# The end of cross attention and the first SwiGLU products, taken in halves of the tokens

## The chip, the cores and the metric

The kernel runs on one core of a Trainium2 chip. The metric is the time of one execution in device microseconds (us). A core has five engines with queues of their own, each of which takes its instructions strictly in its own order: TensorE (PE; its weight loads are listed as PEld), VectorE (DVE), ScalarE (ACT), GpSimd (POOL) and SyncE (SP), which issues most transfers.

## The reference, cut to what matters

Two layers act on 1024 tokens of 1024 features. Each layer is a mixer, then cross attention into 256 memory tokens, then a SwiGLU network of width 2816, each with a root-mean-square norm ahead and a residual add behind. The change is at the seam between the last two.

```python
def rms_norm(x, g):
    y = xf * lax.rsqrt(jnp.mean(xf * xf, axis=-1, keepdims=True) + EPS)
    return (y * g.astype(jnp.float32)).astype(x.dtype)
...
    x = x + memory_cross_attention(rms_norm(x, g_xa[layer]), m, ...)     # ends in  o @ w_o
    x = x + swiglu(rms_norm(x, g_ffn[layer]), w_gate[layer], w_up[layer], w_down[layer])
...
def swiglu(h, w_gate, w_up, w_down):
    return (jax.nn.silu(h @ w_gate) * (h @ w_up)) @ w_down
```

## The kernel before, in words

**Layout.** The residual stream is kept transposed: eight chunks `x[m]` of 128 features (partitions) by 1024 tokens. A fp32 matrix is split in a rounded high part and a low part (`h` and `l`), and a product is three matmuls: high by high, high by low, low by high. The high part is a ScalarE cast (L306 for the activations, L242 for weights), the low part a VectorE subtraction (`low`, L433). "Matmul" below means one such instruction on 128x128 weights and 512 columns.

**SwiGLU in seven products.** Gate and up are done by a seven-product scheme on 2x2 blocks (`seven`, L1749). A `Pair` (L278) holds two neighbouring chunks; its blocks are b11 and b12 (first and second 512 tokens of the even chunk) and b21 and b22 (of the odd one). It yields seven operands: 0 is b11, 1 is b21, 6 is b22, and 2 to 5 are differences of blocks, made by four GpSimd subtractions (L296). A `Unit` is the like for a 1024x256 piece of weights. One product is 12 matmuls: four pairs by three. A gate unit and an up unit are 14 products, and 11 such couples follow each other in a layer.

**The seam.** Cross attention ends in `project(1, m)` (L1660), for chunk after chunk: 12 matmuls for both halves of the tokens, and two VectorE adds onto `x[m]` (L1666). `x_part` (L1722) then makes, for each half, a scaled copy g*x on ScalarE (L1730), which the pair's blocks are taken from, a square on ScalarE (L1734, L1737), and on GpSimd the sum of squares over the chunks (L1738). When a chunk has both halves it is stored to DRAM (L1742) and its buffer is freed. A pair is ready when both of its chunks are through. After product 0 of the first gate unit, `stats` turns the sum of squares into 1/rms with 8 one-column products on TensorE, and `spread` broadcasts it over the partitions. It is needed only where a product's output is gated.

**What sets the order.** A planner (`run`, L447) walks a list of tasks. It makes operands ahead of their task, in the order of first use, as far as a look-ahead in columns (`la`) and room in two SBUF arenas allow; `lead` puts the operands of three pairs ahead of the first product. A scheduler below it then sets each engine's own order. Transfers are issued by SyncE in order.

## Time and profile before

| | before |
|---|---|
| median of 3 runs | 2464.09 us (2460.8 to 2465.05) |
| profiled execution: time, span | 2464.76 us, 2463.0 us |
| TensorE busy | 2355.2 us (96%) |
| VectorE, ScalarE, GpSimd busy | 1729.0 (70%), 1023.0 (42%), 747.0 us (30%) |
| mean granted TensorE clock | 0.977 |

The profiled execution is within 0.7 us of the median, so sums made on its span carry over. A share is a mean over the run: stages differ, and a stage is read from its own stretch. A granted clock of 1.00 is TensorE's upper level of 2.4 GHz, 0.50 the lower of 1.2 GHz; a value between is a mean over the stretch.

### The profile page before, as it was taken

Reading aid. Unit: us, or ns where it says so; the run is one execution under the profiler, and the core shown is the slowest. Engines: PE = TensorE matmul, PEld = TensorE weight load, DVE = VectorE, ACT = ScalarE, POOL = GpSimd, SP = SyncE. Lnnn points to the kernel's source line nnn. Section 1 sums busy time; section 2 is a strip of 40 time slices with the busy share of each in tenths; the row PEclk is TensorE's granted clock in tenths of the full one; section 3 lists DMA queues with packets and bytes.
Section 4 is the critical chain, followed back from the end, with each engine's and each line's share of the span. In section 5 each row is a group of like instructions: output and inputs, shape, how many; then the busy total and the mean of one; then the engine's idle time right before and its main releaser. Section 6 shows DMA issues by size and latency. Waiting matters only on the chain. (4 is left out here: it accounts for less than half of the span.)

```text
span 2463.0 us, 30890 instructions
## 1 busy us (share of the span) xinstructions
PE 2355.2 (96%) x11246; PEld 1973.7 (80%) x11246; DVE 1729.0 (70%) x2501; ACT 1023.0 (42%) x1858; POOL 747.0 (30%) x721
## 2 busy tenths in 40 slices
PE   7999999999899999998999999999799999998999
PEld 7998889888668888776887888888577887876887
DVE  5456467855789988877668653455888889877765
ACT  5355356745544444442224221244544444442221
POOL 6541233343454334241001310142642334331000
PEclk9999999999989999999999999999799999999999
DMA  7345344421214434459762121120314434359773
GB/s 231 125 134 190 95 120 129 129 95 35 103 52 171 154 137 143 165 177 361 261 228 92 57 77 35 35 69 18 120 52 163 149 137 159 133 198 380 235 245 99
DMA packets 249345, 350.24 MB, mean 142 GB/s; under 512 B 13120, under 2 KB 151448, under 8 KB 249192
## 3 DMA queue, kind: packets, MB, share of 16 engines
q1 hardware_dynamic: 245360, 335.46, 41.5%
q0 software_dynamic: 3648, 12.75, 1.4%
q8 instruction: 88, 1.44, 0.2%
q14 instruction: 65, 0.53, 0.1%
q10 hardware_dynamic: 184, 0.05, 0.0%
HBM read 233.78 MB, written 114.43 MB: 141 GB/s over the span
## 5 line engine op out<-in xcount | busy, mean ns | idle before, releaser
L421 PE MATMUL psum_t<-arena_r 128*128 128x512 f32 (+4 forms) x10304 | 2278.4, 380 | 86.3 <-DVE arena_r L433 34.3
L421 PEld LDWEIGHTS psum_t<-arena_r 128*128 128x128 f32 (+1 forms) x10304 | 1863.5, 190 | 451.1 <-DVE arena_r L433 54.2
L433 DVE TENSOR_TENSOR arena_r<-arena_f,arena_r 128x512 fp32r<-128x512 f32 (+4 forms) x811 | 702.8, 886 | 183.1 <-ACT arena_r L242 49.5
L242 ACT CAST arena_r<-arena_f 128x512 fp32r<-128x512 f32 (+2 forms) x504 | 284.0, 584 | 464.1 <-PE psum_t L421 259.0
L1839 POOL TENSOR_TENSOR arena_f<-arena_f 128x512 f32<-128x512 f32 x88 | 164.4, 1875 | 497.5 <-ACT arena_f L1838 497.5
L233 DVE TENSOR_TENSOR arena_f<-arena_f 128x512 f32<-128x512 f32 (+2 forms) x288 | 211.0, 736 | 85.5 <-DMA arena_f<-w_down 52.6
L1818 DVE TENSOR_TENSOR arena_f<-psum_t,arena_f 128x512 f32<-128x512 f32 x224 | 148.1, 684 | 59.3 <-PE psum_t L421 58.6
L1864 ACT CAST arena_r<-arena_f 128x512 fp32r<-128x512 f32 x154 | 95.5, 621 | 197.6 <-DVE arena_f L1846 70.4
L1860 POOL TENSOR_TENSOR arena_f<-arena_f 128x512 f32<-128x512 f32 x88 | 144.0, 1657 | 73.8 <-DVE arena_f L1846 72.1
L1787 DVE TENSOR_TENSOR arena_f<-psum_t,arena_f 128x512 f32<-128x512 f32 x176 | 119.7, 683 | 36.8 <-PE psum_t L421 23.7
L665 POOL TENSOR_TENSOR arena_f<-arena_f 128x1024 f32<-128x1024 f32 x21 | 60.9, 2898 | 273.9 <-ACT arena_f L661 176.0
L551 ACT CAST arena_r<-arena_f 128x1024 fp32r<-128x1024 f32 (+1 forms) x57 | 59.0, 1042 | 114.4 <-PE psum_t L421 97.7
L433 DVE TENSOR_TENSOR arena_r<-psum_t,arena_r 128x512 fp32r<-128x512 f32 (+3 forms) x124 | 84.6, 703 | 23.3 <-ACT arena_r L1653 7.3
L1838 ACT ACTIVATE arena_f<-arena_f 128x512 f32<-128x512 f32 x88 | 55.6, 632 | 83.6 <-DVE arena_f L1837 83.5
L1292 POOL TENSOR_SCALAR arena_f<-arena_f,small 128x640 f32<-128x640 f32 (+6 forms) x64 | 49.5, 782 | 108.7 <-DVE small L1291 104.7
L1846 DVE TENSOR_TENSOR arena_f<-arena_f 128x512 f32<-128x512 f32 x88 | 77.1, 876 | 4.9 <-POOL arena_f L1839 1.2
L444 POOL TENSOR_TENSOR small<-small,mhalf 128x4 f32<-128x4 f32 (+1 forms) x64 | 63.2, 987 | 5.2
L1837 DVE TENSOR_TENSOR arena_f<-arena_f 128x512 f32<-128x512 f32 x88 | 63.3, 720 | 0.1
L1738 POOL TENSOR_TENSOR arena_f<-arena_f 128x512 f32<-128x512 f32 x28 | 43.0, 1551 | 50.6 <-ACT arena_f L1737 50.2
L1287 ACT ACTIVATE arena_f<-psum_t,small 128x640 f32<-128x640 f32 (+6 forms) x64 | 47.5, 744 | 23.2 <-DVE small L1285 20.2
L296 POOL TENSOR_TENSOR arena_f<-arena_f 128x512 f32<-128x512 f32 x32 | 50.8, 1605 | 11.5 <-PE psum_t L421 7.4
L2031 POOL TENSOR_TENSOR arena_f<-arena_f 128x1024 f32<-128x1024 f32 x4 | 10.4, 2601 | 139.6 <-DVE arena_f L1983 134.7
(178 smaller groups left out, 1426.7 us busy)
## 6 DMA issues: line engine op xcount, KB each, us to landing
pq<-arena_r SPq DMA_DIRECT2D x154, 512.0 KB
arena_r<-pq SPq DMA_DIRECT2D x308, 256.0 KB
arena_f<-w_gate SPq DMA_DIRECT2D x22, 1024.0 KB
arena_f<-w_up SPq DMA_DIRECT2D x22, 1024.0 KB
arena_f<-xs SPq DMA_DIRECT2D x32, 512.0 KB
arena_r<-qk SPq DMA_DIRECT2D x48, 256.0 KB
xs<-arena_f SPq DMA_DIRECT2D x24, 512.0 KB
arena_f<-w_down SPq DMA_DIRECT2D x12, 1024.0 KB
```

What stands on the lines that cost most here:

```text
L233: getattr(T.nc, self.adds).tensor_tensor(out=out, in0=a, in1=b, op=what)
L242: T.nc.scalar.copy(out=hv, in_=src)
L421: self.nc.tensor.matmul(out=out, lhsT=lhsT, rhs=rhs, start=start, stop=stop, skip_group_check=again)
L433: getattr(self.nc, eng).tensor_tensor(out=out, in0=src, in1=high, op=ALU.subtract)
L444: self.nc.gpsimd.tensor_tensor(out=out, in0=in_, in1=self.mhalf[:, 0:in_.shape[-1]], op=ALU.pow)
L1787: nc.vector.tensor_tensor(out=o, in0=bank[q].ap, in1=o if other is None else other, op=ALU.add)
L1818: nc.vector.tensor_tensor(out=o, in0=bank[q].ap, in1=o, op=ALU.add)
L1837: nc.vector.tensor_tensor(out=q, in0=q, in1=r, op=ALU.mult)
L1839: nc.gpsimd.tensor_tensor(out=q, in0=q, in1=r, op=ALU.mult)
L1846: nc.vector.tensor_tensor(out=c[j].ap[:, o], in0=c[j].ap[:, o], in1=s.ap[:, o], op=ALU.mult)
L1860: nc.gpsimd.tensor_tensor(out=out, in0=a, in1=b, op=ALU.subtract)
L1864: nc.scalar.copy(out=t.ap[:, 0:512], in_=src)
```

## The change

**Cross attention.** The eight `project(1, m)` are done for the first 512 tokens of all chunks, then for the second 512 (6 matmuls each). `x_final` takes the place of `x_part`. Each half of a chunk is stored by its own transfer, 16 a layer instead of 8, of half the bytes. There is no scaled copy. For a first half, x is scaled in place on GpSimd (after its store has read it), and the sum of squares still runs on GpSimd. For a second half, x stays unscaled, its square goes into four one-column products on TensorE, which write to a PSUM bank of their own.

**Operands.** Operands 0 and 1 of a pair need only the two first halves, the other five need the second halves too. The two first differences are made on VectorE, in an instruction that multiplies by g and subtracts, two others stay on GpSimd; operand 6 is scaled in its cast (ScalarE) and its low part (VectorE).

**Order of the first couple.** Products 0 and 1 of gate and up come first (48 matmuls), then the statistics, then the other ten. The look-ahead is 16384 columns over the seam instead of 3072 and then 2048.

```diff
 class Pair:
+    def ready(self, i):
+        return self.lo[i] if i < 2 else all(self.hi)
...
     def make(self, T, i, h, l):
...
         if i == 2:
-            self.t1, self.t2 = T.F.get(512, "ba"), T.F.get(512, "ba")
-            op(self.t1.ap, b12, b11)
-            op(self.t2.ap, b22, self.t1.ap)
+            nc.vector.scalar_tensor_tensor(out=t1, in0=x12, scalar=self.g[0], in1=b11,
+                                           op0=ALU.mult, op1=ALU.subtract)
+            nc.vector.scalar_tensor_tensor(out=t2, in0=x22, scalar=self.g[1], in1=t1,
+                                           op0=ALU.mult, op1=ALU.subtract)
         if i == 4:
-            op(b12, b22, b12)
+            nc.gpsimd.tensor_tensor(out=t1, in0=t2, in1=b11, op=ALU.subtract)
         if i == 5:
-            op(b21, b21, self.t2.ap)
+            nc.gpsimd.tensor_tensor(out=t2, in0=b21, in1=t2, op=ALU.subtract)
+        if i == 6:
+            nc.scalar.activation(out=h.ap, in_=x22, func=AF.Copy, scale=self.g[1])
+            nc.vector.scalar_tensor_tensor(out=l.ap, in0=x22, scalar=self.g[1], in1=h.f,
+                                           op0=ALU.mult, op1=ALU.subtract)
...
-        for m in range(8):
-            self.add(lambda m=m: project(1, m, wo[1][m // 4]), [wo[1][m // 4]])
+        def tail():
+            self.la, self.f_reserve = 16384, 1024
+        self.add(tail)
+        for half in range(2):
+            if half:
+                self.add(lambda: setattr(self, "f_reserve", 4096))
+            for m in range(8):
+                self.add(lambda m=m, half=half: project(1, m, wo[1][m // 4], (half,)), [wo[1][m // 4]])
...
-    def x_part(self, pairs, gname, layer, m, half):
+    def x_final(self, pairs, layer, m, half):
...
+        nc.sync.dma_start(out=self.xs[m * P:(m + 1) * P, c], in_=x)
+        if half:
+            pr.hi[e] = True
...
+            def sums():
+                for b in range(4):
+                    self.mm(self.sums.ap[:, m * 4 + b:m * 4 + b + 1], sq.ap[:, b * P:(b + 1) * P],
+                            self.ones[:, 0:1], True, True)
...
+        def scale():
+            nc.gpsimd.tensor_scalar(out=x, in0=x, scalar1=pr.g[e], scalar2=1.0, op0=ALU.mult, op1=ALU.mult)
+            pr.lo[e] = True
+        self.defer(scale, 2)
...
+                lead = [p.ops[i] for p in pairs[:2] for i in (2, 3, 6, 4, 5)]
+                gt = self.seven(g, pairs, self.collected(later(gated)), lead)
+                ut = self.seven(u, pairs, self.collected(later(upped(0))))
+                self.tasks += gt[:2] + ut[:2]
+                self.add(lambda: (self.half_stats(), self.spread()))
+                self.tasks += gt[2:]
+                self.add(steady)
+                self.tasks += ut[2:]
```

**TensorE, layer 0, from the last transposes of cross attention on.** Before (`128x1` are the one-column products of the statistics, `arena_f,ones` the broadcast):

```order
L421 MATMUL psum_t<-arena_r 128x512 x159
L421 MATMUL psum_t<-ones,arena_f 128x1 x4
L421 MATMUL psum_t<-arena_r 128x512 x4
L421 MATMUL psum_t<-ones,arena_f 128x1 x4
L421 MATMUL psum_t<-arena_r 128x512 x11
L421 MATMUL psum_t<-arena_f,ones 128x512 x2
L421 MATMUL psum_t<-arena_r 128x512 x2813
```

And now:

```order
L442 MATMUL psum_t<-arena_r 128x512 x122
L442 MATMUL psum_t<-ones,arena_f 128x1 x4
L442 MATMUL psum_t<-arena_r 128x512 x5
L442 MATMUL psum_t<-ones,arena_f 128x1 x4
L442 MATMUL psum_t<-arena_r 128x512 x20
L442 MATMUL psum_t<-ones,arena_f 128x1 x8
L442 MATMUL psum_t<-arena_r 128x512 x38
L442 MATMUL psum_t<-ones,arena_f 128x1 x8
L442 MATMUL psum_t<-arena_r 128x512 x13
L442 MATMUL psum_t<-ones,arena_f 128x1 x12
L442 MATMUL psum_t<-arena_r 128x512 x42
L442 MATMUL psum_t<-arena_f,ones 128x512 x2
```

Four batches of 12 more matmuls stand ahead of the statistics, and 32 one-column products are spread among them where there were none.

**VectorE, layer 0, from the first adds of `project(1, m)` on.** L1666 is now L1696 (add onto x), L433 is now L454 (low part), L313 and L323 are the new scaled subtractions. Before:

```order
L1666 TENSOR_TENSOR arena_f<-psum_t,arena_f 128x512 x5
L433 TENSOR_TENSOR arena_r<-arena_f,arena_r 128x512
L1666 TENSOR_TENSOR arena_f<-psum_t,arena_f 128x512 x2
L433 TENSOR_TENSOR arena_r<-arena_f,arena_r 128x512 x2
L1666 TENSOR_TENSOR arena_f<-psum_t,arena_f 128x512 x2
L433 TENSOR_TENSOR arena_r<-arena_f,arena_r 128x512
L1666 TENSOR_TENSOR arena_f<-psum_t,arena_f 128x512 x2
L433 TENSOR_TENSOR arena_r<-arena_f,arena_r 128x512 x2
L1666 TENSOR_TENSOR arena_f<-psum_t,arena_f 128x512 x2
L433 TENSOR_TENSOR arena_r<-arena_f,arena_r 128x512
L1666 TENSOR_TENSOR arena_f<-psum_t,arena_f 128x512 x2
L433 TENSOR_TENSOR arena_r<-arena_f,arena_r 128x512 x14
```

And now:

```order
L454 TENSOR_TENSOR arena_r<-arena_f,arena_r 128x512
L1696 TENSOR_TENSOR arena_f<-psum_t,arena_f 128x512
L233 TENSOR_TENSOR arena_f<-arena_f 128x4x128
L454 TENSOR_TENSOR arena_r<-arena_f,arena_r 128x512 x2
L1696 TENSOR_TENSOR arena_f<-psum_t,arena_f 128x512 x5
L454 TENSOR_TENSOR arena_r<-arena_f,arena_r 128x512
L1696 TENSOR_TENSOR arena_f<-psum_t,arena_f 128x512 x2
L454 TENSOR_TENSOR arena_r<-arena_f,arena_r 128x512
L1696 TENSOR_TENSOR arena_f<-psum_t,arena_f 128x512
L454 TENSOR_TENSOR arena_r<-arena_f,arena_r 128x512
L1696 TENSOR_TENSOR arena_f<-psum_t,arena_f 128x512
L323 SCALAR_TENSOR_TENSOR arena_r<-arena_f,gc,arena_r 128x512
```

The first row now is the low part of chunk 0's first half. It and the low part of chunk 1's stand ahead of the adds of chunks 2 to 6 (`x5`), the next low part ahead of the add of chunk 7, and the last add of the second halves stands twelve rows below these, behind the first scaled subtractions. Before, all adds stood ahead of a block of 14 low parts.

**GpSimd, layer 0, over the seam.** L1738 is now L1788 (sum of squares), L296 is now L318 and L320 (differences), L1793 is the scaling in place. Before:

```order
L1738 TENSOR_TENSOR arena_f<-arena_f 128x512 x10
L296 TENSOR_TENSOR arena_f<-arena_f 128x512
L1738 TENSOR_TENSOR arena_f<-arena_f 128x512
L296 TENSOR_TENSOR arena_f<-arena_f 128x512 x2
L1738 TENSOR_TENSOR arena_f<-arena_f 128x512 x2
L296 TENSOR_TENSOR arena_f<-arena_f 128x512 x2
L1738 TENSOR_TENSOR arena_f<-arena_f 128x512
L296 TENSOR_TENSOR arena_f<-arena_f 128x512 x5
L444 TENSOR_TENSOR rstd<-small,mhalf 128x8
L296 TENSOR_TENSOR arena_f<-arena_f 128x512 x6
```

And now:

```order
L1793 TENSOR_SCALAR arena_f<-arena_f,gc 128x512 x2
L1788 TENSOR_TENSOR arena_f<-arena_f 128x512
L1793 TENSOR_SCALAR arena_f<-arena_f,gc 128x512
L1788 TENSOR_TENSOR arena_f<-arena_f 128x512
L1793 TENSOR_SCALAR arena_f<-arena_f,gc 128x512 x2
L1788 TENSOR_TENSOR arena_f<-arena_f 128x512
L1793 TENSOR_SCALAR arena_f<-arena_f,gc 128x512 x2
L1788 TENSOR_TENSOR arena_f<-arena_f 128x512
L1793 TENSOR_SCALAR arena_f<-arena_f,gc 128x512
L1788 TENSOR_TENSOR arena_f<-arena_f 128x512 x3
L318 TENSOR_TENSOR arena_f<-arena_f 128x512
L320 TENSOR_TENSOR arena_f<-arena_f 128x512
```

Eight of sixteen differences and seven of fourteen sums are gone; eight scalings come among the sums, and the sums stand ahead of all differences.

## Rows read from the trace of the kernel before

**Rows 1.** Stretches of 100 us: length, engines' busy us (instructions), granted clock, DMA.
```profile
core 0: us, PE busy (x) PEld busy (x) DVE busy (x) ACT busy (x) POOL busy (x), PEclk, DMA share, GB/s
...
600.00:700.00 100.00, 85.01 (x357) 65.25 (x356) 73.89 (x92) 51.29 (x95) 54.87 (x48) 0.83 0.24 85
700.00:800.00 100.00, 99.90 (x439) 81.88 (x438) 89.49 (x119) 46.79 (x81) 35.87 (x22) 1.00 0.37 126
800.00:900.00 100.00, 99.93 (x441) 82.34 (x440) 88.87 (x116) 45.74 (x80) 37.15 (x22) 1.00 0.42 146
...
1700.00:1800.00 100.00, 80.69 (x334) 62.40 (x333) 79.47 (x88) 48.97 (x93) 52.84 (x42) 0.85 0.21 74
```

**Rows 2.** The same by stretches around the two stalls, TensorE alone.
```profile
627.83:662.09 34.26, 34.26 (x153) 1.00 0.31 123
662.09:696.69 34.60, 19.62 (x44) 0.55 0.30 91
696.69:727.20 30.51, 30.41 (x125) 0.95 0.06 20
1725.57:1753.03 27.46, 27.46 (x123) 1.00 0.22 87
1753.03:1804.76 51.73, 30.65 (x93) 0.70 0.29 97
1804.76:1826.80 22.04, 22.04 (x90) 0.92 0.07 25
```

**Rows 3.** Groups by line and shape, 600-705 us: busy, mean; idle before, releaser.
```profile
L433 DVE TENSOR_TENSOR arena_r<-arena_f,arena_r 128x512 fp32r<-128x512 f32 x34 | 35.0, 1053 | 10.7 <-ACT arena_r L306 10.1
L296 POOL TENSOR_TENSOR arena_f<-arena_f 128x512 f32<-128x512 f32 x16 | 25.2, 1601 | 0.0
L1666 DVE TENSOR_TENSOR arena_f<-psum_t,arena_f 128x512 f32<-128x512 f32 x32 | 21.2, 685 | 7.2 <-PE psum_t L421 7.0
L1738 POOL TENSOR_TENSOR arena_f<-arena_f 128x512 f32<-128x512 f32 x14 | 20.9, 1506 | 33.5 <-ACT arena_f L1737 33.4
L306 ACT CAST arena_r<-arena_f 128x512 fp32r<-128x512 f32 x28 | 16.9, 613 | 13.9 <-POOL arena_f L296 13.9
L1730 ACT ACTIVATE arena_f<-arena_f,gc 128x512 f32<-128x512 f32 x16 | 11.1, 714 | 9.3 <-DVE arena_f L1666 9.3
```

**Rows 4.** Timeline of GpSimd (POOL), 655 to 690 us: start, length, line, operands, count.
```profile
657.21 1.29 POOL L1738 TENSOR_TENSOR arena_f<-arena_f 128x512 f32<-128x512 f32 x1 [3.15 <-ACT arena_f L1737]
662.09 6.31 POOL L1738 TENSOR_TENSOR arena_f<-arena_f 128x512 f32<-128x512 f32 x4 [3.59 <-ACT arena_f L1737]
```

**Rows 5.** Timeline of VectorE (DVE), 655 to 690 us.
```profile
657.82 1.29 DVE L1666 TENSOR_TENSOR arena_f<-psum_t,arena_f 128x512 f32<-128x512 f32 x2 [0.80 <-PE psum_t L421]
659.03 3.09 DVE L433 TENSOR_TENSOR arena_r<-arena_f,arena_r 128x512 fp32r<-128x512 f32 x5
662.56 4.72 DVE L433 TENSOR_TENSOR arena_r<-arena_f,arena_r 128x512 fp32r<-128x512 f32 x3 [0.44 <-ACT arena_r L306]
```

**Rows 6.** Groups by line and shape, whole run, GpSimd.
```profile
L1292 POOL TENSOR_SCALAR arena_f<-arena_f,small 128x512 f32<-128x512 f32 x8 | 5.5, 691 | 11.2 <-DVE small L1291 11.1
```

**Rows 7.** Groups by line and shape, whole run, VectorE.
```profile
L653 DVE SCALAR_TENSOR_TENSOR arena_r<-arena_f,gc,arena_r 128x1024 fp32r<-128x1024 f32 x24 | 41.7, 1742 | 8.7 <-ACT arena_r L652 8.6
...
L2035 DVE SCALAR_TENSOR_TENSOR arena_f<-arena_f,gc 128x1023 f32<-128x1023 f32 x4 | 5.1, 1284 | 14.5 <-ACT arena_f L2033 14.5
```

**Rows 8.** Last line on tensor xs, then on qk: its transfers' landing times, us.
```profile
DMA to landing us min/median/max: 3.9/5.1/7.5
...
DMA to landing us min/median/max: 3.2/4.0/6.6
```

**Rows 9.** Timeline of TensorE, 540 to 550 us: one-column products at full clock.
```profile
542.32 1.84 PE L421 MATMUL psum_t<-ones,arena_f 128*128 128x1 f32 x16
```

More of the change, by code (lines that the diff above doesn't have):

```diff
@@ L252 @@
     cols = 512
+    heavy = False
     def __init__(self, pair, i):
         self.pair, self.i = pair, i
-        self.heavy = i == 0
         self.left = 0
     def ready(self):
-        return self.pair.ready
+        return self.pair.ready(self.i)
     def fetch(self, T, must):
-        return self.i > 0 or self.pair.fetch(T, must)
+        return self.i != 2 or self.pair.fetch(T, must)
     def make(self, T, must):
@@ L283, in __init__ @@
     def __init__(self):
-        self.t = [None, None]
-        self.ready = False
+        self.x, self.g = [None, None], [None, None]
+        self.lo, self.hi = [False, False], [False, False]
+        self.made = 0
         self.ops = [Operand(self, i) for i in range(7)]
+    def ready(self, i):
+        return self.lo[i] if i < 2 else all(self.hi)
     def fetch(self, T, must):
+        if not self.ready(2) and not must:
+            return False
+        t1 = T.F.alloc(512, "ba")
+        t2 = t1 and T.F.alloc(512, "ba")
+        if t2 is None:
+            if t1:
+                t1.free()
+            assert not must, ("sums", T.F.map())
+            return False
+        self.t1, self.t2 = t1, t2
@@ L1737, in x_part, with more, half_stats, seven @@
             nc.scalar.activation(out=sq.ap, in_=x, func=AF.Square)
[L1738 to L1749 removed]
+            def more():
+                nc.gpsimd.tensor_tensor(out=self.ssq.ap, in0=self.ssq.ap, in1=sq.ap, op=ALU.add)
+                sq.free()
+            self.defer(more)
+        def scale():
+            nc.gpsimd.tensor_scalar(out=x, in0=x, scalar1=pr.g[e], scalar2=1.0, op0=ALU.mult, op1=ALU.mult)
+            pr.lo[e] = True
+        self.defer(scale, 2)
+    def half_stats(self):
+        nc = self.nc
+        ps = self.sums
+        for b in range(4):
+            self.mm(ps.ap[:, 32 + b:33 + b], self.ssq.ap[:, b * P:(b + 1) * P], self.ones[:, 0:1], True, True)
+        t = self.tiny(8)
+        nc.vector.tensor_reduce(out=t[:, 4:8], in_=ps.ap[:, 0:32].rearrange("p (m b) -> p b m", b=4),
+                                op=ALU.add, axis=AX.X)
+        nc.vector.tensor_scalar(out=t[:, 0:4], in0=ps.ap[:, 32:36], scalar1=1.0 / D, scalar2=EPS,
+                                op0=ALU.mult, op1=ALU.add)
+        nc.vector.tensor_scalar(out=t[:, 4:8], in0=t[:, 4:8], scalar1=1.0 / D, scalar2=EPS,
+                                op0=ALU.mult, op1=ALU.add)
+        self.rpow(self.rstd, t)
+        ps.free()
+        self.ssq.free()
+        self.ssq = None
+    def seven(self, unit, pairs, after, lead=()):
         bank = {}
@@ L1767, in fn @@
             after(i, bank)
-        for i in range(7):
-            ws = list(lead) if i == 0 else []
-            self.add(lambda i=i: fn(i), ws + [unit.parts[i]] + [p.ops[i] for p in pairs])
-            if then:
-                then(i)
+        return [Task(lambda i=i: fn(i), [unit.parts[i]] + (list(lead) if i == 2 else []) + [p.ops[i] for p in pairs])
+                for i in range(7)]
     def collected(self, quarter, where="ba"):
@@ L1780, in after @@
             if i == 0:
-                st["c"] = [self.F.get(S, where) for _ in range(2)]
+                st["c"] = []
+            if i in (0, 4):
+                st["c"].append(self.F.get(S, where))
             c = st["c"]
@@ L1851, in upped, with later, fn @@
             return fn
+        def later(quarter):
+            def fn(j, half, c):
+                if (j, half) == (0, 0):
+                    self.defer(lambda: quarter(j, half, c), 5)
+                else:
+                    quarter(j, half, c)
+            return fn
         def store(pr, c):
```

94 lines of the change are left out of this document (49 added, 45 removed).

## The prediction, as written before the result was known

> **What bounds the kernel now.** I first read the run by stretches [rows 1]. From 700 to 900 us TensorE is busy for over 99.9 of each 100 us at the upper clock, and 441 matmuls take 100 us, 0.227 us each: there the kernel is bound by TensorE. Two stretches stand out, 600 to 700 and 1700 to 1800, with 85.0 and 80.7 us busy and a clock of 0.83 and 0.85. Both hold the seam that the change rebuilds. Closer [rows 2]: in layer 0 TensorE runs without a gap to 662.1; then 34.6 us hold only 44 instructions (24 matmuls, 16 one-column passes, 4 passes of the broadcast) at a clock of 0.55; then it is full again. In layer 1 the bad stretch is 51.7 us long with 93 instructions (73 of them matmuls).
>
> What holds it there is the making of operands. GpSimd is the slow link: 16 differences (25.2 us) and 14 sums of squares (20.9 us) [rows 3]; the casts wait 13.9 us for the differences, and the low parts 10.1 us for the casts. GpSimd and VectorE also hold each other up. A low part takes 0.62 us alone (five in 3.09) and 1.57 beside a GpSimd sum (three in 4.72), and that sum takes 1.29 alone and 1.58 in such company [rows 4, 5]. An add that has one operand in PSUM is not touched: two take 1.29 us beside the sum at 657.2.
>
> **The most that can come back.** Count from the start of the last gapless run to the end of the fourteenth product of the first couple. By the program's order that is 300 matmuls in layer 0 (132 to the first product, then 168) and 282 in layer 1 (114 and 168). It takes 34.26 + 34.60 + 30.51 = 99.4 us and 27.46 + 51.73 + 22.04 = 101.2 us [rows 2]. TensorE alone would need 300 x 0.227 = 68.1 and 64.0 us, plus the statistics. These grow: 36 one-column products instead of 8, two passes each; 16 passes took 1.84 us, 0.115 each [rows 9], so 72 take 8.3 us where 16 take 1.8, and 6.4 us more stand on TensorE's path in each layer. With 2 us of broadcast the floors are 78.4 and 74.3, the gains at most 21 and 27 us, and the time at best 2464.8 - 48 = 2417.
>
> **The change part by part.** ScalarE: 16 scaled copies of 0.714 us go; it is not the last to finish, so this counts for nothing by itself. GpSimd: 7 sums and 8 differences go, 8 scalings of about 0.69 [rows 6] come; 46 us become about 29. VectorE: eight differences come, as scaled subtractions. The nearest rows give 0.64 per 512 columns alone and 0.87 in company [rows 7]; I take 0.7, so 5.6 us are added. In return 15 fewer two-input GpSimd instructions run beside it, each of which costs it 1.57 - 0.62 = 0.95: 14 us less. What is last next is therefore VectorE, and its order decides.
>
> The page "SBUF — State Buffer" of the Trainium skill (section "Who interferes with whom") says that of a VectorE instruction with two SBUF inputs and a GpSimd one that reads SBUF the later blocks until the first is done. By that a pair would take 0.62 + 1.29 = 1.91 us, and the end would come at 2452; the rows show 1.57, and by them it comes at 2442. My sum goes by the rows; the other is a rival below.
>
> **A new wait.** The scaling in place must wait until the store has read the half. Behind it in their queues wait the other scalings, sums and differences (GpSimd), the squares (ScalarE) and, behind the first low part, the adds of chunks 2 to 7 (VectorE). The trace has no 256 KB store of x. The nearest rows are the 512 KB ones, 3.9 to 7.5, median 5.1, and the transfers of qk, 256 KB, median 4.0 [rows 8]; I take 4.5 and keep 3.2 and 7.5 for the range. One hop (store, scaling 0.7, cast 0.6, low part 0.7) is 6.5 us.
>
> **Layer 0, from the start of the run.** Chunk 0's first half is done after 28 matmuls, 6.4 us, and added at 7.1. First hop: its low part ends at 13.6. Chunk 2's add stands five instructions behind, 16.8. Second hop: its low part ends at 23.3, and chunk 7's add, which stands behind it, at 24.0. Chunk 7's low part stands 14 VectorE instructions after that add: 7 adds at 0.65 and about 8 others at 1.2 (half of them beside GpSimd) make 14 us, which also covers the third hop. So the first-half operands are complete at 38. TensorE comes to them at 132 x 0.227 + 1.8 = 31.8 and runs most of the four batches meanwhile, so it waits some 3 us. From 38 on, 39 VectorE instructions stand up to the low part of the last operand: 39 x 0.64 = 25 and 8 differences on GpSimd x 0.95 = 7.6, so 71 us. By then the order lets TensorE do 93 of the 168 matmuls; it is short of operands for much of that, and I expect the lower clock again. Then 75 matmuls (17.0), the broadcast (2) and some 3 us until the clock is back: 93 us against 99.4. Gain 6.
>
> **Layer 1.** The same sum, with 18 matmuls less ahead (4.1 us) and four first-half adds ahead of the first low part instead of two: one hop less, of whose 6.5 us I take 4, since the adds of the second halves then queue sooner. The last operand is at 63, the end at 85 against 101.2. Gain 16, because before lost more here.
>
> Nothing eats this later: at 700 to 900 us TensorE is full with VectorE at 89%, and the weights are loaded ahead as before. The sum: 2464.8 - 22 = 2442.
>
> **The rivals.** (a) *Near the floor*: stores land in 3.2 us (three hops and two, 1.3 each: 6.5 us), GpSimd costs VectorE half as much (15 x 0.5 a layer, less what falls into its pauses: some 8 us in all) and the clock does not fall (3 a layer): 2442 - 20 = 2422. For it: the stores are half as large. Against it: VectorE's order is full to the last operand.
>
> (b) *The full lock*: each of the 15 two-input GpSimd instructions costs VectorE its 1.29 alone [rows 4] instead of 0.95, 5 us a layer, 10 in all: 2452. The pairs of 1.57 [rows 5] speak against it. It is the rule of the Trainium skill's page "SBUF — State Buffer" named above.
>
> (c) *Nothing left*: the cover is spent, because VectorE comes out of the seam with the outputs of the first couple still to gate and the weights of the second to make, and TensorE waits for weight parts that wait for VectorE. At 89% the reserve is 11 us in 100, so a backlog of about 20 instructions (13 us) a layer stays with it; of 22 us some 2 remain: 2462. For it: VectorE's order puts gating right behind the last operand.
>
> (d) *Slower*: the hops decide. If the stores land in 7.5 us, three hops cost 9 us more in layer 0 and two 6 in layer 1. TensorE then waits inside the projection, the clock is down from there on, and 40 of the last 75 matmuls run at half of it: 9 us, 6 more than counted. The squares of the second halves, behind casts that wait for the scalings, hold up the one-column products, which stand in TensorE's order ahead of matmuls that could run: 4 us a layer. Layer 0 ends at 112, 13 later than before, layer 1 at 101, the same: 2478. It decides once a hop is above some 9 us. Against it: the store's median is 5.1.
>
> That the products do not begin early is no rival: in the built order 48 more matmuls stand ahead of the statistics.
>
> **How the numbers follow.** Forecast 0.44, (a) 0.14, (b) 0.13, (c) 0.14, (d) 0.15. The likeliest is the sum, 2442. A measurement of this kernel tells some 0.2%, 5 us, from no change. Faster by more: forecast, (a) and (b), 0.71; within it: (c), 0.14; slower: (d), 0.15. The range is 2424 to 2470: it holds the forecast with its bounds, (b) and (c), and leaves out half of (a) and nearly all of (d), 0.2 in all.
>
> **What would show it.** TensorE: 48 matmuls with no wait for a low part right after the projection; then a stretch at a clock below 1.00, shorter than 34.6 and 51.7 us, whose end is released by VectorE's low parts and no longer by GpSimd's differences. VectorE busy nearly without a gap through it. GpSimd's scalings start 4 to 5 us after their adds. The one-column products take about 8 us a layer. The forecast is wrong if TensorE waits inside the projection (d), if the clock stays at 1.00 (a), or if the seam is shorter and waits appear in the couples behind it (c).

## The result, and the profile after

| | before | after |
|---|---|---|
| median | 2463.84 us (2460.8 to 2465.05, 4 runs) | 2441.28 us (2437.37 to 2444.03, 4 runs) |
| profiled execution: time, span | 2464.76, 2463.0 us | 2443.61, 2441.5 us |
| mean granted TensorE clock | 0.977 | 0.986 |

The ratio is 0.9914, with a 95% interval of 0.9899 to 0.9928: 22.6 us less by the medians, 21.5 by the spans, where 22 were forecast. The parts that make it up are not the forecast ones.

The busy times by stage show it. The stages are cut at fixed matmuls: TensorE runs the same 10304 f32r matmuls in both kernels, so the n-th of them marks the same point of the work. The stretches are layer 0's seam (start of the gapless run to the end of the first couple, 300 matmuls), couple 2, couples 3 to 7, couples 8 to 11, layer 1's seam (282 matmuls), and its couples 2 to 11. First the kernel before:

```profile
core 0: us, PE busy (x) PEld busy (x) DVE busy (x) ACT busy (x) POOL busy (x), PEclk, DMA share, GB/s
627.83:727.98 100.15, 85.07 (x324) 63.42 (x322) 77.57 (x94) 53.60 (x93) 53.11 (x35) 0.83 0.23 82
727.98:766.06 38.08, 38.08 (x170) 31.53 (x168) 35.67 (x47) 17.46 (x32) 14.61 (x9) 1.00 0.49 171
766.06:957.66 191.60, 190.99 (x842) 157.50 (x840) 170.99 (x227) 88.62 (x156) 73.56 (x40) 1.00 0.44 152
957.66:1121.88 164.22, 156.59 (x674) 126.10 (x672) 128.67 (x177) 70.49 (x129) 55.23 (x32) 0.99 0.51 173
1725.57:1826.67 101.10, 80.01 (x305) 60.56 (x303) 84.75 (x90) 53.09 (x92) 54.87 (x34) 0.83 0.22 78
1826.67:2227.49 400.82, 388.89 (x1681) 315.71 (x1680) 344.35 (x457) 175.89 (x316) 142.41 (x81) 0.99 0.47 161
```

And the same stretches after the change:

```profile
628.78:715.87 87.09, 83.96 (x380) 69.08 (x378) 75.30 (x100) 43.56 (x74) 35.41 (x26) 0.94 0.26 89
715.87:758.82 42.95, 40.30 (x169) 32.47 (x168) 37.82 (x51) 18.26 (x34) 19.89 (x10) 0.96 0.40 140
758.82:957.69 198.87, 193.18 (x842) 156.92 (x840) 169.54 (x225) 88.31 (x156) 70.93 (x40) 1.00 0.42 146
957.69:1120.01 162.32, 155.09 (x674) 125.12 (x672) 130.15 (x177) 70.57 (x127) 54.40 (x32) 1.00 0.52 179
1722.86:1809.89 87.03, 81.49 (x361) 65.50 (x359) 72.34 (x96) 43.55 (x74) 37.15 (x26) 0.92 0.29 96
1809.89:2207.75 397.86, 387.55 (x1682) 317.07 (x1680) 340.57 (x454) 178.93 (x318) 142.80 (x83) 0.99 0.46 159
```

Read the first number behind each stretch. The seams are 13.1 and 14.1 us shorter, with the granted clock up from 0.83 to 0.94 and 0.92. But in layer 0 couple 2 takes 4.9 us more and couples 3 to 7 take 7.3 more: 12.1 of the 13.1 us are gone by 957.7, where both kernels are at the same point at the same time (957.66 and 957.69). Couples 8 to 11 take 1.9 us less, so that layer 0 keeps 2.8 us in all. In layer 1 nothing is lost behind the seam; the couples there take 3.0 us less. So in this profile **layer 1 carries the result, and layer 0 gives most of its gain back**. On the page, TensorE's group of f32r matmuls now idles 18.3 us for low parts in all, where before it was 34.3 (before, then after):

```profile
L421 PE MATMUL psum_t<-arena_r 128*128 128x512 f32 (+4 forms) x10304 | 2278.4, 380 | 86.3 <-DVE arena_r L433 34.3
L442 PE MATMUL psum_t<-arena_r 128*128 128x512 f32 (+4 forms) x10304 | 2270.7, 379 | 67.0 <-DVE arena_r L454 18.3
```

TensorE's timeline of layer 0's seam answers [rows 2] (start, duration, operation, count, idle time ahead and its releaser; shown are the rows with a wait, and one other):

```profile
675.77 1.95 PE L442 MATMUL psum_t<-ones,arena_f 128*128 128x1 f32 x16 [1.08 <-ACT arena_f L1771]
...
680.49 1.20 PE L442 MATMUL psum_t<-arena_r 128*128 128x512 f32 x4 [1.28 <-DVE arena_r L454]
682.40 1.77 PE L442 MATMUL psum_t<-arena_r 128*128 128x512 f32 x3 [0.72 <-ACT arena_r L327]
683.98 5.11 PE L442 MATMUL psum_t<-ones,arena_f 128*128 128x1 f32 x24
...
730.19 1.24 PE L442 MATMUL psum_t<-arena_r 128*128 128x512 f32 x4 [0.56 <-ACT arena_r L242]
733.53 1.69 PE L442 MATMUL psum_t<-arena_r 128*128 128x512 f32 x4 [2.09 <-DVE arena_r L454]
```

TensorE does not wait inside the projection; its first wait begins 46 us after the start of the run, and the waits of the seam are 3.1 us together where before they were 15.1. The last two rows are already couple 2: there it waits again, for a ScalarE cast and for VectorE, and behind the second wait the granted clock is at 0.50 from 734.0 to 737.4. That lowers couple 2's mean to 0.96, an estimate of 1.7 us of the 4.9.

**What VectorE waits for.** The main waits of VectorE and TensorE in couples 2 to 7, in total, number and longest (L1787, now L1852, is the add that empties a PSUM bank, L1797 and L1862 are ScalarE's copies out of one); first before, then after:

```profile
DVE arena_f L1787 <- PE psum_t L421: 9.0, 5, 2.7
DVE arena_r L433 <- ACT arena_r L242: 4.3, 6, 0.9
DVE arena_f L1787 <- ACT arena_f L1797: 3.9, 3, 2.1
DVE arena_r L433 <- ACT arena_r L1864: 1.5, 4, 0.7
DVE arena_f L233 <- DMA arena_f<-w_gate: 1.2, 1, 1.2
DVE arena_f L233 <- DMA arena_f<-w_up: 0.8, 2, 0.5
PE psum_t L421 <- DVE arena_r L433: 0.5, 1, 0.5
```
```profile
DVE arena_f L233 <- DMA arena_f<-w_gate: 7.9, 3, 4.9
PE psum_t L442 <- DVE arena_r L454: 7.0, 9, 2.1
DVE arena_f L1852 <- PE psum_t L442: 6.4, 4, 2.2
DVE arena_r L454 <- ACT arena_r L242: 5.5, 5, 3.0
DVE arena_r L454 <- ACT arena_r L1937: 4.8, 5, 1.8
DVE arena_f L1852 <- ACT arena_f L1862: 3.7, 2, 2.3
DVE arena_f L233 <- DMA arena_f<-w_up: 3.5, 2, 2.8
```

Before, VectorE waits 2.0 us for weight loads (w_gate, w_up), 9.7 for ScalarE's casts and copies and 9.4 for TensorE. After, it waits 11.4 us for loads and 14.0 for ScalarE, and TensorE waits 7.0 us for low parts. VectorE's work is the same: by the rows of couples 2 to 7 above it is busy for 206.7 us before and 207.4 after. What has grown is the time in which it stands idle, from 23.0 to 34.5 us, nearly as much as the couples have lost. VectorE takes its instructions strictly in order, so while its head instruction stands, low parts that could be made stand behind it. One such place, on VectorE, on the queue of loads and on TensorE:

```profile
831.36 0.69 DVE L233 TENSOR_TENSOR arena_f<-arena_f 128x512 f32<-128x512 f32 x1
831.96 1.90 DVE L454 TENSOR_TENSOR arena_r<-arena_f,arena_r 128x512 fp32r<-128x512 f32 x3
838.75 1.42 DVE L233 TENSOR_TENSOR arena_f<-arena_f 128x512 f32<-128x512 f32 x2 [4.89 <-DMA arena_f<-w_gate]
```
```profile
832.68 0.37 SPq L223 DMA_DIRECT2D arena_f<-w_gate  x1
```
```profile
840.82 13.89 PE L442 MATMUL psum_t<-arena_r 128*128 128x512 f32 x60 [1.90 <-DVE arena_r L454]
```

The first of the three low parts at 831.96 is the last reader of the place into which the load goes, so the load leaves at 832.68, and the first sum on it starts at 838.75, 6.1 us later. The built order has only two VectorE instructions between that low part and the first sum on the new weights (L233). At some 0.65 us each they fill 1.3 of the 6.1 us, and VectorE stands still for 4.9; TensorE then waits 1.9 us for a low part. The same happens at 700.0, still in the seam (one instruction between, 4.2 us), and 825.9 (four, 2.8 us). In the order of before the numbers in this stretch are 8, 6, 6, 7, 5, 6, 5 and 4, and VectorE stands for 1.2 us at most.

### The profile page after: what moved, and what is told of

The parts are those of the page before. It is cut to its first block, busy times and chain, and to the rows that moved or that the text cites. A ratio compares the mean times of both kernels' runs of the same rounds, so it can differ in the third digit from the quotient of the medians.

```text
span 2441.5 us, 31142 instructions
## 1 busy us (share of the span) xinstructions
PE 2356.0 (96%) x11358; PEld 1984.2 (81%) x11358; DVE 1714.9 (70%) x2521; ACT 1008.5 (41%) x1826; POOL 712.3 (29%) x707
## 4 chain that ended last, share of the span: by engine, by line
PE 70%; DVE 14%; DMA 8%; issue 4%; ACT 2%; POOL 1%; SPq 0%; DVEq 0%; ACTq 0%; POOLq 0%
PE psum_t L442 67%; DVE arena_r L454 7%; DMA pq<-arena_r 2%; DMA arena_f<-w_gate 2%; DVE arena_f L233 1%; DVE arena_f L1852 1%; DMA arena_f<-w_up 1%; PE psum_t L1323 1%; DMA arena_f<-w_down 1%; DMA arena_r<-pq 1%; DVE arena_f L1911 1%; ACT arena_r L242 1%; DVE arena_f L1883 1%; DMA arena_f<-e_w_in 1%; PE psum_t L1646 1%
## 5 line engine op out<-in xcount | busy, mean ns | idle before, releaser
L442 PE MATMUL psum_t<-arena_r 128*128 128x512 f32 (+4 forms) x10304 | 2270.7, 379 | 67.0 <-DVE arena_r L454 18.3
L454 DVE TENSOR_TENSOR arena_r<-arena_f,arena_r 128x512 fp32r<-128x512 f32 (+4 forms) x803 | 672.7, 858 | 181.8 <-ACT arena_r L242 49.0
L1904 POOL TENSOR_TENSOR arena_f<-arena_f 128x512 f32<-128x512 f32 x88 | 160.4, 1828 | 488.5 <-ACT arena_f L1903 488.5
L233 DVE TENSOR_TENSOR arena_f<-arena_f 128x512 f32<-128x512 f32 (+2 forms) x288 | 208.6, 728 | 91.8 <-DMA arena_f<-w_down 50.9
L1933 POOL TENSOR_TENSOR arena_f<-arena_f 128x512 f32<-128x512 f32 x88 | 144.5, 1661 | 88.4 <-DVE arena_f L1911 64.7
L1937 ACT CAST arena_r<-arena_f 128x512 fp32r<-128x512 f32 x154 | 95.5, 621 | 175.2 <-DVE arena_f L1911 64.2
L1852 DVE TENSOR_TENSOR arena_f<-psum_t,arena_f 128x512 f32<-128x512 f32 x176 | 119.4, 683 | 36.5 <-PE psum_t L442 19.6
L454 DVE TENSOR_TENSOR arena_r<-psum_t,arena_r 128x512 fp32r<-128x512 f32 (+3 forms) x124 | 84.5, 703 | 21.7 <-ACT arena_r L1650 7.9
L1306 DVE TENSOR_REDUCE small<-psum_t 128x1 f32<-128x640 f32 (+5 forms) x64 | 47.2, 750 | 7.5 <-PE psum_t L442 7.1
L1636 POOL TENSOR_SCALAR arena_f<-arena_f,small 128x256 f32<-128x256 f32 x64 | 30.4, 495 | 68.3 <-DVE small L1633 58.9
```

Of the source, the lines that this page charges most:

```text
L233: getattr(T.nc, self.adds).tensor_tensor(out=out, in0=a, in1=b, op=what)
L442: self.nc.tensor.matmul(out=out, lhsT=lhsT, rhs=rhs, start=start, stop=stop, skip_group_check=again)
L454: getattr(self.nc, eng).tensor_tensor(out=out, in0=src, in1=high, op=ALU.subtract)
L1852: nc.vector.tensor_tensor(out=o, in0=bank[q].ap, in1=o if other is None else other, op=ALU.add)
L1904: nc.gpsimd.tensor_tensor(out=q, in0=q, in1=r, op=ALU.mult)
L1933: nc.gpsimd.tensor_tensor(out=out, in0=a, in1=b, op=ALU.subtract)
```

## The experiments

Each edit changes more than its place: the scheduler orders every queue anew, so VectorE's order shifts in the rest of the program too. The stages of all profiled executions stand therefore side by side (us; seam 0 and seam 1 are those of layers 0 and 1, couples without a layer are layer 0's, and "stands" is VectorE's waiting in layer 0's couples 2 to 7, for weight loads + for ScalarE). The first 2924 matmuls, ahead of the seam, take 612.0 to 615.9 us in the 14 profiles, which says how far single executions differ by themselves: VectorE's order there is the same in all 14 but for the last instructions. In layer 0 before and layer1_only have the same VectorE order, and their stages agree within 0.3 us up to couple 7 and within 1.1 us behind it.

| kernel | median, ratio to before | seam 0 | couple 2 | couples 3-7 | couples 8-11 | seam 1 | layer 1, couples 2-11 | stands |
|---|---|---|---|---|---|---|---|---|
| before | 2463.8 | 100.1 | 38.1 | 191.6 | 164.2 | 101.1 | 400.8 | 2.0 + 9.7 |
| after | 2441.3, 0.9914 [0.9899, 0.9928] | 87.1 | 43.0 | 198.9 | 162.3 | 87.0 | 397.9 | 11.4 + 14.0 |
| layer0_only | 2445.8, 0.9932 [0.9920, 0.9945] | 85.1 | 42.9 | 198.2 | 162.2 | 97.4 | 393.8 | 12.7 + 13.9 |
| layer1_only | 2445.6, 0.9930 [0.9917, 0.9942] | 100.1 | 38.1 | 191.9 | 165.3 | 87.2 | 397.5 | 1.3 + 9.7 |
| g1_low_region | 2437.8, 0.9907 [0.9893, 0.9921] | 87.0 | 43.0 | 192.3 | 163.4 | 87.0 | 400.7 | 4.1 + 12.9 |
| more_stock | 2424.1, 0.9844 [0.9830, 0.9857] | 85.2 | 39.4 | 197.4 | 164.8 | 81.2 | 395.0 | 11.9 + 10.2 |
| stock_and_place | 2429.9, 0.9867 [0.9847, 0.9887] | 87.1 | 39.4 | 199.4 | 157.9 | 81.4 | 399.6 | 15.2 + 11.9 |
| stock_and_place_both | 2432.8, 0.9883 [0.9865, 0.9901] | 85.2 | 39.4 | 199.4 | 157.0 | 82.9 | 399.5 | 12.2 + 12.0 |
| gate_then_up | 2433.1, 0.9876 [0.9862, 0.9891] | 90.0 | 38.1 | 193.0 | 167.9 | 87.4 | 393.6 | 3.0 + 9.6 |
| squares_on_gpsimd | 2428.9, 0.9860 [0.9843, 0.9876] | 89.0 | 39.8 | 192.5 | 162.9 | 85.6 | 394.1 | 5.7 + 13.3 |
| projection_by_chunks | 2439.6, 0.9904 [0.9890, 0.9917] | 88.2 | 41.1 | 191.4 | 162.7 | 87.6 | 399.7 | 3.9 + 12.0 |
| differences_on_gpsimd | 2439.3, 0.9901 [0.9888, 0.9915] | 87.9 | 42.0 | 198.8 | 163.0 | 86.3 | 399.3 | 11.5 + 11.0 |
| gate_then_up_and_squares | 2446.0, 0.9933 [0.9920, 0.9947] | 95.7 | 39.4 | 195.1 | 163.0 | 92.1 | 399.7 | 2.4 + 15.3 |
| some_stock | 2450.8, 0.9952 [0.9939, 0.9964] | 87.2 | 41.6 | 205.2 | 180.3 | 83.1 | 395.9 | 5.6 + 22.3 |

The expectations cut the stages a little earlier, at matmuls 3188, 3400 and 4200 instead of the ends of couples 1, 2 and 7 (3224, 3392, 4232), and at 7412 and 7680 in layer 1 instead of 7418 and 7700; where a number of theirs is met or missed, the value at their cut is given.

**The layers apart.** A kernel with both forms of the seam, chosen by layer (the diffs of this section are cut to the lines that matter, at "...").

```diff
...
-            if pr == 1:
+            if pr == 1 and layer not in NEW:
+                self.x_part(pairs, "ffn", layer, m, half)
+            if pr == 1 and layer in NEW:
                 self.x_final(pairs, layer, m, halves[0])
...
```

> The change in layer 0 alone; layer 1 is as in the kernel before. Theory A (the two seams add up, and layer 0 gives its gain back behind the seam): the n-th matmul at the end of layer 0's couples stands where it stood before, within 2 us, and the time is 2461, 2 to 4 below before. Rival B (the layers share the gain; layer 0's lead is only shifted about by what layer 1 does): about half of the gain, 2453.

> The change in layer 1 alone. Theory A: nearly all of the gain is layer 1's, 18 to 19 us, 2445. Rival B: about half, 2453.

Layer 1 alone gives 2445.6, as theory A said. Layer 0 alone gives 2445.8, which neither theory had. Its own part is as in the changed kernel: the seam 15.0 us shorter, couples 2 to 7 11.4 longer. Layer 0's couples end 5.7 us earlier than in before (1116.2 against 1121.9), where A had at most 2. What is new stands in layer 1, whose source is that of before:

```profile
1716.40:1813.84 97.44, 78.68 (x305) 59.81 (x304) 80.09 (x90) 52.94 (x93) 53.35 (x35) 0.82 0.23 83
1813.84:2207.63 393.79, 386.94 (x1681) 314.86 (x1680) 337.88 (x448) 173.28 (x310) 137.74 (x81) 1.00 0.47 163
```

These two stretches take 3.7 and 7.0 us less than in the kernel before, with the same work in the same lines; VectorE's and ScalarE's orders in them are others. So an edit 1000 us away moves a layer by 10.7 us, and the single gains, 16.8 and 17.0 us against a median of 2462.6 for before, do not add up to the 22 of both.

**Where layer 0's gain goes.** Two edits of the changed kernel, alone and together, then a value in between. The second edit moves two numbers: the columns kept free (`reserve`), and the look-ahead (`la`), from 2048 to 3072. The value in between, some_stock, keeps 2048 columns free in layer 0 and has the look-ahead of 3072 in both layers.

```diff
-            g = Unit(wg, 0, 4, j * 256, "b" if j == 10 else "ba")
+            g = Unit(wg, 0, 4, j * 256, "b" if j == 10 else "ab" if (layer, j) == (0, 1) else "ba")
```
```diff
         def steady():
-            self.reserve, self.la = 3072, 2048
+            self.reserve, self.la = 1024 if layer == 0 else 3072, 3072 if layer == 0 else 2048
```

> The changed kernel, where the gate weights of layer 0's second couple are loaded into the lower half of the f32 arena, which is free earlier, instead of a place that overlaps the first couple's gate weights. Theory C (layer 0 loses its lead because these weights land at 700 us and VectorE stands still for them with the low parts behind them in its queue): no wait of 4 us on VectorE at 700, TensorE loses some 5 us less by 740 us, and part of it lasts: 2434 to 2437. Rival D (VectorE's backlog of the seam is the cause, whatever lands when): the lead is given back by 950 us all the same, 2439 to 2443.

> The changed kernel, where in layer 0's couples after the first the planner keeps 1024 columns of the operand arena free instead of 3072, so that weight parts may be made further ahead. Theory D (a backlog of VectorE, with no stock behind the seam): parts further ahead cost the same VectorE time, so nothing comes back before 950 us, and the time is 2440 to 2443. Theory E (TensorE waits for single late parts because the stock is thin): waits for low parts between 730 and 950 us fall from 8 us to under 3, 2434 to 2437.

With the other place, VectorE still stands 3.9 us in the seam, now for up weights, and couple 2 takes 43.0 as without the edit: theory C is wrong on couple 2. Couples 3 to 7 take 192.3, with 4.1 us of standing for loads instead of 11.4, so that 7.5 us of the seam's lead are left behind couple 7: D is wrong too. The time, 2437.8, lies within the spread of the changed kernel, since layer 1's couples, which the edit does not touch, take 2.8 us more.

With more stock couple 2 takes 39.4 instead of 43.0, and TensorE's wait for low parts there falls from 2.1 to 0.9 us, which goes with theory E: the parts of the second couple were made late because the planner did not make them far enough ahead. It held in both other kernels with 1024 columns (39.4 each); with 2048 columns and the same look-ahead couple 2 takes 41.6, so the columns count, and what the look-ahead adds is not shown. From 730 to 950 us the waits for low parts fall from 7.0 to 3.4 us, where E had under 3, and couples 3 to 7 gain 1.5 us only. The kernel is 17 us below the changed one, further than either theory had it, and 8.7 of these are layer 1's (81.2 and 395.0), which the edit does not touch. It is the fastest that was run, 38 us below before; of the 17, layer 0's couples 2 to 7, where its edit acts, give 5.1.

> Both edits of the runs before in layer 0 alone: the second couple's gate weights in the lower half of the f32 arena, and 1024 instead of 3072 columns kept free. Theory F (layer 0's lead goes in two pieces: the second couple stalls because its parts are made late for want of room, and the next ones because VectorE stands still for weights that land late): both pieces are saved, matmuls 3188 to 3400 take 49 us as with more stock and 3400 to 4200 take 183 as with the other place, where before took 230.6 in all and the changed kernel 242.7; 2418 to 2426. Rival G (one cause in two guises: VectorE has a backlog to work off, and what is saved in one piece is lost in the other): 236 or more for these matmuls, 2424 to 2436.

> The same, and the 1024 columns in layer 1 too. Theory F: layer 1's couples lose 2 us less; within 4 us of the run with the edits in layer 0 alone, 2415 to 2425. Rival G: as there, 2424 to 2436.

Couple 2 is saved again, couples 3 to 7 (199.4) are not: matmuls 3400 to 4200 take 190.4 where F wanted 183, and VectorE stands 15.2 us for loads. In the new order the place no longer helps. F's second half falls, and G's figures are met: 239.7 us for matmuls 3188 to 4200 in both kernels (236 or more), and both times lie in its range. In layer 1 the stock changes nothing (399.5 against 399.6).

> The changed kernel with 2048 columns kept free in layer 0's couples after the first, between the changed kernel's 3072 and the 1024 of more_stock. In its built order the loads behind the first have 8, 6, 4, 7, 5, 8, 10 and 8 VectorE instructions between the freeing low part and the first sum, where the changed kernel has 8, 10, 6, 7, 4, 2 and more_stock 9, 8, 4, 3, 3, 4. Theory M: matmuls 3188 to 3400 take 49 to 50 us (stock), 3400 to 4200 take 183 to 186 (VectorE stands for weights under 9 us); 2428 to 2436. Rival G (backlog): 3400 to 4200 take 188 or more, as in more_stock and the changed kernel.

Theory M fails here: 51.6 and 196.1 us at the expectation's cuts, 2450.8 in all; G's 188 or more is met. VectorE stands for loads only 5.6 us, as its order promised, but 22.3 for ScalarE. Two waits of this kernel from 715 to 1110 us, one of VectorE and one of TensorE:

```profile
DVE arena_r L454 <- ACT arena_r L1937: 32.1, 13, 7.0
...
PE psum_t L442 <- DVE arena_f L1852: 13.1, 7, 2.4
```

and TensorE's timeline, with a period of one couple:

```profile
899.76 40.35 PE L442 MATMUL psum_t<-arena_r 128*128 128x512 f32 x168 [1.99 <-DVE arena_f L1852]
941.13 3.47 PE L442 MATMUL psum_t<-arena_r 128*128 128x512 f32 x14 [1.02 <-DVE arena_f L1852]
945.48 35.32 PE L442 MATMUL psum_t<-arena_r 128*128 128x512 f32 x154 [0.89 <-DVE arena_r L454]
982.80 3.47 PE L442 MATMUL psum_t<-arena_r 128*128 128x512 f32 x14 [1.99 <-DVE arena_f L1852]
```

Here low parts of stored operands, which wait for ScalarE's cast (L1937), stand ahead of the adds that free TensorE's banks (L1852), couple after couple. So loads are one head of the queue, casts another. Taken together, the sum of the last column follows the time of couples 2 to 7 over the 14 kernels: 11 to 13 us of standing with 229.7 to 231.1 us, 16 to 19 with 232.3 to 235.3, 22 to 28 with 236.8 to 246.7 (rank correlation 0.92; for loads alone the linear correlation is 0.65, for the sum 0.92). VectorE's busy time in these couples is 204.4 to 208.8 us in all 14, whatever they take. So what differs between the kernels is not how much VectorE has to do, as a backlog (G) would have it, but how long it stands.

How a place in the order costs time can be read from the 118 loads in these couples whose freeing VectorE instruction the 14 traces tell. With one or two instructions between it and the first sum, the sum waits for its load 4.8 us in the mean (4.0 to 5.4), with three 2.3, with four 1.1, with five or six 0.6, with seven or more 0.2. It is a slope and not a threshold: with four to six the single wait is anything from 0 to 4.0 us.

Behind couple 7 the link is weaker. In couples 8 to 11 the same sum has a linear correlation of 0.59 with the time, and loads alone have -0.32; before itself stands 17.8 us for loads there. In couples 2 to 7, on the other hand, before had an order in which TensorE waits 0.6 us in all, while layer 1's ten couples cost it 11.9 us before and 10.3 after. One reading, which no run tests, is that layer 0 lost an unusually good order.

**Parts undone.** The first couple in the order of before; the squares of the second halves on GpSimd (the statistics are then 8 one-column products); both.

```diff
-                self.tasks += gt[:2] + ut[:2]
+                self.tasks += gt[:2]
                 self.add(lambda: (self.half_stats(), self.spread()))
                 self.tasks += gt[2:]
                 self.add(steady)
-                self.tasks += ut[2:]
+                self.tasks += ut
```
```diff
...
             def sums():
-                for b in range(4):
-                    self.mm(self.sums.ap[:, m * 4 + b:m * 4 + b + 1], sq.ap[:, b * P:(b + 1) * P],
-                            self.ones[:, 0:1], True, True)
+                nc.gpsimd.tensor_tensor(out=self.ssq2.ap, in0=self.ssq2.ap, in1=sq.ap, op=ALU.add)
...
```

> The changed kernel with the first couple's products in the order of before (all seven of gate, then all seven of up; the statistics stand after the second product). Theory A: VectorE makes the last operand as late as in the changed kernel, and 24 matmuls less are done by then, 5.5 us a layer: 2451. Rival H (TensorE is short of operands up to the last one in either order, and the early products only fill a stretch that would be filled by others): 2441.

> The changed kernel with the squares of the second halves summed on GpSimd, as those of the first halves are, and 8 one-column products instead of 36. Theory A (VectorE is the bound of the seam, and a two-input GpSimd instruction costs it 0.95 us): 7 more of them a layer, 6.6 us on VectorE and some 10 on GpSimd ahead of the differences: 2451 to 2457. Rival I (the one-column products are the price, 56 passes of 0.115 us a layer, and more at half the clock): 6.4 us less a layer, 2428 to 2434.

> Both parts undone that cost nothing alone: the first couple's products in the order of before, and the squares of the second halves summed on GpSimd. In its built order most weight loads have more than 6 VectorE instructions between the low part that frees their place and the first sum on them. Theory M (VectorE's standing for weights, where fewer than about 8 instructions lie between, is what gives the gain back): matmuls 3188 to 4200 take 231 to 234 us, the seams 82 to 85 us each: 2424 to 2433. Rival G (a shorter seam is paid back by VectorE's backlog): the seams are longer, so less comes back, and the sum of seam and couples is the changed kernel's 321.6 us in layer 0; 2437 to 2443.

Undoing the order costs the seams 2.9 and 0.4 us, not 5.5 each, and yet the kernel is faster than the changed one, and than H's 2441: couples 2 to 7 take 231.1 instead of 241.8, and couples 8 to 11 give 5.6 of that back (167.9 instead of 162.3). The squares on GpSimd cost 1.9 and gain 1.4. Rival I has the time right (2428.9) and its reason wrong: the seams are not 6 us shorter, the couples are (232.3). VectorE's busy time in layer 0's seam rises from 75.3 to 83.1 us, 1.1 for each of the seven sums if all of it is theirs, close to the forecast's 0.95; TensorE has 56 one-column passes less, and the seams show the two nearly in balance. Both undone, the seams are 95.7 and 92.1 us, 8.6 and 5.1 longer, far more than the two alone:

```profile
627.46:723.11 95.65, 80.75 (x324) 62.90 (x322) 88.63 (x104) 45.38 (x77) 50.72 (x35) 0.86 0.32 108
```

VectorE is busy for 88.6 of 95.7 us there, 13.3 more than in the changed kernel, and TensorE has lost both fillers, the early up products and the one-column products; its waits in this stretch are 14.9 us again. The run does not tell the one from the other. M's range for the couples, 231 to 234 at its cuts, was missed by 1.5 us (235.5), its range for the seams, 82 to 85, by 2.5 and 4.7 (87.5, 89.7), and its time by 13. G came nearer: seam and couples are 323.0 us in layer 0 (321.6), and the time is 3 us above its range.

Then the projection by chunks (two conditions of the planner go with it), and the first differences on GpSimd, where ScalarE scales the second halves in place.

```diff
...
-        for half in range(2):
...
-            for m in range(8):
+        for m in range(8):
+            for half in range(2):
                 self.add(lambda m=m, half=half: project(1, m, wo[1][m // 4], (half,)), [wo[1][m // 4]])
...
```
```diff
-            nc.vector.scalar_tensor_tensor(out=t1, in0=x12, scalar=self.g[0], in1=b11,
-                                           op0=ALU.mult, op1=ALU.subtract)
...
+            nc.gpsimd.tensor_tensor(out=t1, in0=x12, in1=b11, op=ALU.subtract)
...
```

> The changed kernel with the projection chunk by chunk again, both halves of a chunk one after the other, and everything else as changed. Theory K (what shortens the seam is that the first halves are done early: their operands are made while TensorE still projects): the first-half operands are complete only when the projection has ended, and matmuls 2924 to 3188 take 86 to 92 us instead of 78.9, 7412 to 7680 92 to 98 instead of 84.7; 2452 to 2462. Rival L (it is the differences moved to VectorE, in any order of the halves): 77 to 81 and 83 to 87 us.

> The changed kernel with both first differences of each pair on GpSimd again, eight a layer; the second halves are scaled in place by ScalarE for it. Theory L (the differences on GpSimd were the bound): 8 x 1.3 to 1.6 us more on GpSimd behind the second halves, 10 to 13 us; VectorE gets 5.6 less and 7.6 more. The seams grow by 6 to 10 us each, 85 to 89 and 91 to 95 us; 2453 to 2461. Rival K (the order by halves carries the gain): within 3 us, 2438 to 2446.

Neither theory survives both runs. By chunks the seams take 80.1 and 85.2 us at the expectation's cuts, as the order by halves does (78.9, 84.7): K falls. With the differences on GpSimd they take 79.8 and 83.9, where L had 85 to 89 and 91 to 95: L falls too. The seam's row of the second:

```profile
627.79:715.73 87.94, 83.45 (x379) 67.29 (x378) 74.38 (x91) 47.85 (x81) 48.20 (x34) 0.94 0.26 90
```

GpSimd is busy for 48.2 instead of 35.4 us, and the seam is 0.8 us longer. One thing more: VectorE's order behind this seam has the same distances between freeing low part and sum as the changed kernel's (1, 8, 8, 6, 7, 4, 2 against 1, 8, 10, 6, 7, 4, 2), and couples 3 to 7 take 198.8 against 198.9.

## Why the prediction came out where it did

The time was right, 2442 against 2441, but not by its own sum: that it came out so near is luck. Two steps were off by some 6 and 12 us in opposite directions; smaller ones make up the rest (layer 1's seam 2 us longer than forecast, its couples 3 and layer 0's last four 2 us shorter than before).

**Layer 1's seam**: forecast 85 us, measured 87.0. The last operand, forecast for 63 us after the start of the run, was there at 64.7 (VectorE's low part ends at 1787.6). Mechanism and size were right.

**Layer 0's seam**: forecast 93, measured 87.1. First-half operands complete at 35.6 us (38), last operand at 65.9 (71), then 21.2 us (22). Of the 5 us by which the last operand came early, 2.4 lie ahead of the first-half operands and 2.7 behind them, where 39 VectorE instructions and 8 differences took 30.3 us instead of 33. Ahead of them the mis-sized term is the store. I took 4.5 us for it, from the landings of other transfers [rows 8]; the scaling in place starts 2.2 to 2.3 us after the store's issue:

```profile
644.92 0.32 SPq L1765 DMA_DIRECT2D xs<-arena_f  x1
```
```profile
647.11 0.69 POOL L1793 TENSOR_SCALAR arena_f<-arena_f,gc 128x512 f32<-128x512 f32 x1 [0.17 <-DVE arena_f L1696]
```

(also 636.37 to 638.69, and in layer 1 1738.87 to 1741.15 and 1743.97 to 1746.22). The page "DMA: Bandwidth & Descriptors" of the Trainium skill (section "Anatomy of one DMA — SWDGE (gpsimd) path") gives 2.0 us and the bytes by 436 GB/s, an estimate of 2.6 us for 256 KB; it is for another issuing path, but it was nearer than my rows. Two hops at the measured price come 4.5 us earlier, so something else ahead of the first-half operands was some 2 us longer than forecast; what it was stays open.

**"Nothing eats this later"** is the step that failed. It was drawn from VectorE's share of 89% and from the weights being "loaded ahead as before"; in layer 0's couples 2 to 7 VectorE stood 11.4 us for them instead of 2.0. Rival (c) came true in layer 0, to 12.1 of 13.1 us by couple 7, and not in layer 1. Its reason was wrong, however: it spoke of a backlog that VectorE works off with 11% to spare, as G did in the experiments. G's figures were met in three runs and nearly in a fourth, but its mechanism was not: VectorE's busy time in couples 2 to 7 is the same in all 14 kernels, and seam 0 with these couples is no fixed sum (320.8 to 333.9 us, before 329.8). projection_by_chunks has nearly the same seam and keeps nearly all of the gain (232.5 us in couples 2 to 7, before 229.7, and 162.7 in couples 8 to 11); gate_then_up keeps it as far as couple 7 (231.1) and half of it behind couple 11. What decides is the place of single instructions in VectorE's order: the fewer stand between the freeing low part and the first sum, the longer the sum stands for its load, and low parts stand behind it. That VectorE stands for a load and TensorE waits behind it is shown by the rows at 838 us; that this makes up the loss is supported by kernels of equal distances with equal couples, and by the 14 kernels together up to couple 7. It is not proven: a run that takes only the standing away was not made, since each edit gives another order.

**What GpSimd does.** The forecast called it the bound of before, removed by moving differences and sums. Either alone can go back for 1.9 us or less. It stays open which part carries the 13 and 14 us; taking both fillers from TensorE, with the load on VectorE that comes with it, costs 8.6 and 5.1, and no run undid the planner's look-ahead over the seam or the folded scales.

**The other rivals.** (a) came nearest to the store (3.2 us), but not to the rest: a GpSimd sum did not get cheaper for VectorE (1.1 us), and the clock falls to a mean of 0.74 from 680 to 700. (d) fell with the store: TensorE does not wait in layer 0's projection, and only 0.5 us in layer 1's. (b), the full lock, was priced a little high (1.29 us each) and rejected for the wrong reason; the last section has its rows. The one-column products take 10.8 us in layer 0 (24 of the 72 passes at the lower clock level, 5.11) and 8.25 in layer 1, where I had 8.3.

## What to carry to other kernels

Follow a gain to the end of the program: cut both traces at the same matmuls, and look where the lead shrinks. Behind a shortened stretch the next limit may be the order of one in-order queue; count the instructions between what frees a buffer and the first reader of its next load, and compare their time with the load's. Before a stall is called a backlog, compare the engine's busy time: a backlog is more work, standing is not. Where a scheduler orders all queues anew, a verdict on one edit has a spread of its own (here 2424 to 2451 us among twelve near relatives), so read an edit from the stage that it touches and not from the total alone.

## What the runs showed of the hardware

In the changed kernel 220 VectorE instructions of 512 columns with two SBUF inputs start while GpSimd is in a two-input one. Of these, 166 end some 0.55 us after GpSimd does, wherever in its instruction they began. GpSimd, then VectorE:

```profile
669.98 1.60 POOL L320 TENSOR_TENSOR arena_f<-arena_f 128x512 f32<-128x512 f32 x1 [0.70 <-DVE arena_r L454]
674.23 2.16 POOL L318 TENSOR_TENSOR arena_f<-arena_f 128x512 f32<-128x512 f32 x1 [2.65 <-DVE arena_f L315]
```
```profile
670.36 1.77 DVE L323 SCALAR_TENSOR_TENSOR arena_r<-arena_f,gc,arena_r 128x512 fp32r<-128x512 f32 x1
...
672.66 0.74 DVE L313 SCALAR_TENSOR_TENSOR arena_f<-arena_f,gc 128x512 f32<-128x512 f32 x1
...
675.18 1.75 DVE L323 SCALAR_TENSOR_TENSOR arena_r<-arena_f,gc,arena_r 128x512 fp32r<-128x512 f32 x1
```

GpSimd ends at 671.58 and 676.39, VectorE at 672.13 and 676.93; alone, an instruction of this kind takes 0.74. Another 48 run in their own 0.68 us, all inside GpSimd instructions that take 1.8 to 5.8 us instead of the 1.29 that they take alone: there GpSimd waits for VectorE. So either waits for the other. That agrees with the exclusive lock of the page "SBUF — State Buffer" of the Trainium skill (section "Who interferes with whom"). What it costs VectorE is the rest of GpSimd's instruction, not the whole of it, which is how a lock and the forecast's 0.95 a piece go together.
